# First group of a hybrid decoder step, layer 0: the norm factor moves from the input to the evictions, and its statistic behind the first unit of products

## The chip, the core and the metric

The kernel runs on one core of one Trainium2 chip. The metric is the device time of one execution in microseconds; the median of three runs before the change is 2014.07 us (2012.44 to 2017.64).

## The reference, cut to what matters

The reference makes one inference step of a two-layer decoder for 1024 prompt tokens and 64 sample tokens. Layer 0, the one that is changed, is

```python
proj = rms_norm(x, norm_g) @ w_in            # x * rsqrt(mean(x*x) + EPS) * g
u, gb, gc, q_mem, z = split(proj)
conv = sum(conv_w[j] * full[:, j:j+t] for j in range(3))   # full: history, then gc * u
q = rms_norm(q_mem, mem_q_g)                 # per head
out = concat(gb * conv, mem_attend(q, k, v)) * silu(z)
y = x + out @ w_out
```

The keys and values of the memory, for both layers, come from `rms_norm(mem, norm_g) @ w_kv`. Layer 1 (latent attention) has the same shape of input projection and is not changed.

## The kernel before, in words

**Products.** All large products are made in three passes: `split` (L183, L179) cuts each operand into a high half on ScalarE and a low half on VectorE (or POOL), and `mm3` (L188 to L191) adds high by high, high by low and low by high in PSUM. Data lie with features on the partitions and tokens in the free dimension. Group A has 320 tokens (256 of the prompt and the 64 samples), group B the other 768 in two chunks of 384. A unit is 128 output features: eight steps of the contraction in `fm`, three products each, so 24 products per chunk. A PSUM tile for it comes from a ring of three (`mmt`).

**Weights.** `Stream` loads the weights of a unit on SP's queue, splits them, and keeps two units in both forms; `get(i)` splits unit i + 1 and issues the load of i + 2. The first unit comes in four pieces (L297). For the memory weights (`mem_kv`, 8 units of 2048 columns over two layers) `M_ENG` names the engine of the low half unit by unit: `"vvgv"` gives units 2 and 6 to POOL, the others to VectorE.

**Group A, layer 0** (`group_a`). Four DMAs load `x`. `norm_T` squares the eight blocks on ScalarE (L250, L258), adds them on VectorE (L259), then `norm_T2` takes the statistic: `stat_r` sums over partitions on TensorE (L214), scales on VectorE (L220), and finds the inverse root by an integer guess and three Newton steps of tiny instructions (`rsqrt_`, L202 to L206). `bcast_tok` puts the factor on a diagonal (L233) and multiplies it with ones on TensorE (L234), so that PSUM holds the factor of each token on all partitions. Each block is then scaled (`xnxa`, L272) and split into `xH` and `xL` (L183, L179). Only then can `in0` make its first product.

`in0` runs over 40 units: conv blocks 0 to 3 of four units each (`u`, gc, z, gb), then four memory heads of two units each (`mem_part`: query and gate), then conv blocks 4 to 7, with the attention of the samples over their memory beside them. In a conv block, `u` is copied out of PSUM on ScalarE (L654), gc is multiplied with it (L659), three multiply-adds make the convolution `cv`, z is turned into its gate by `silu2` (tanh on ScalarE, L608, and one instruction on VectorE, L609), `cv` is multiplied by it (L678), and gb by that (L682). In layer 1 the same helpers already work with a factor `rb` that is multiplied in at the eviction: L605 in `silu2`, L452 for the query's sum of squares, and `split_g` (L239, L240) makes the halves of the input with the gain but without the factor.

**Order.** Two streams of work are written by generators, and `interleave` merges them by the costs that they yield: on the left `mem_kv`, group B, prompt attention and the end; on the right group A, then the samples' attention. A right cost is multiplied by 0.8 in the first part (`RAT`), by 0.6 from the memory heads of group A on. So at the start `mem_kv` (5.2 for its first unit, then 2.6 per half unit) is merged with group A: the squares yield 0.48 each, the statistic `NY` = 7.0, the broadcast 3.0, the eight scaled blocks 0.64 each, and a unit 3.2. Group B's squares, statistic and scaled blocks come after `mem_kv`, beside group A's memory heads. The merged order sets priorities; a planner then puts the instructions on each engine's queue, where they run in order.

Of the kernel before, what the change touches and what calls it, by code (L numbers as in the profile page):

```python
# [5 lines left out]
F = mybir.dt.float32  # L6
# [5 lines left out]
AF = mybir.ActivationFunctionType  # L12
ALU = mybir.AluOpType
# [3 lines left out]
D = 1024  # L17
# [7 lines left out]
EPS = 1e-6  # L25
# [23 lines left out]
KL = list(range(6, 12)) + list(range(6))  # L49
NATB = 4  # L50
RECB = 2
M_ENG = ("vvgv", "a")
A_ENG = ("v", "a")
SCL = "vaaaaaaa"
PSP = "ggg"
# [2 lines left out]
NY = 7.0  # L58
# [27 lines left out]
VG0, VG1, VGM, VGQL, VGQ, VGK, VMQ, VCW = 0, 8, 16, 32, 35, 36, 37, 39  # L86
# [6 lines left out]
def build(nc, tc, I, O):  # L93
# [94 lines left out]
    def mm3(out, wh, wl, xh, xl, first, last):  # L188
        T.matmul(out, wh, xh, start=first, stop=False)  # L189
        T.matmul(out, wh, xl, start=False, stop=False)  # L190
        T.matmul(out, wl, xh, start=False, stop=last)  # L191

    cnt = [0]
    sm = {}
# [43 lines left out]
    def split_g(h, l, x, c):  # L238
        A.activation(h, x, AF.Copy, scale=vcol(c))  # L239
        V.scalar_tensor_tensor(out=l, in0=x, scalar=vcol(c), in1=h.bitcast(F), op0=ALU.mult, op1=ALU.subtract)  # L240
# [87 lines left out]
    def fm(ps, n, w, nk, xH, xL, c0):  # L328

        wh, wl = w  # L330
        for k in range(nk):
            mm3(ps[:, 0:n], wh[:, k * 128:(k + 1) * 128], wl[:, k * 128:(k + 1) * 128], xH[:, k, c0:c0 + n], xL[:, k, c0:c0 + n], k == 0, k == nk - 1)


    def mem_kv(side=None):
# [90 lines left out]
    def mem_part(l, g, pp, ws, qi, xH, xL, ydst, done, pq, rb=None, fill=None):  # L426
# [9 lines left out]
        def qpart(h, d):  # L436

            assert sm["kv"] >= l
            kr = pp.tile([128, 512], F, name="mraw", tag="mraw", bufs=1)
            S.dma_start(out=kr[:, 0:256], in_=d_kT[l][:, h, :])  # L440
            S.dma_start(out=kr[:, 256:512].rearrange("p (k d) -> p k d", k=2), in_=d_v[l][:, :, h * 128:(h + 1) * 128])
            qH = pp.tile([128, g.np], R, name="mqH", tag="mqH", bufs=2 if g.sample else 1)
            qL = pp.tile([128, g.np], R, name="mqL", tag="mqL", bufs=2 if g.sample else 1)
            sqt = pp.tile([128, g.T], F, name="msq", tag="msq", bufs=1)
            w = ws.get(qi + 2 * h)
            for c0, n in g.chunks:
                ps = mmt()
                fm(ps, n, w, 8, xH, xL, c0)
                yield 0.01 * n
                A.activation(sqt[:, c0:c0 + n], ps[:, 0:n], AF.Square)  # L450
                if l:
                    V.scalar_tensor_tensor(out=sqt[:, c0:c0 + n], in0=acc1[g][:, c0:c0 + n], scalar=EPS * 128 / D, in1=sqt[:, c0:c0 + n], op0=ALU.mult, op1=ALU.add)  # L452
                m = max(0, min(n, g.np - c0))
                split(qH[:, c0:c0 + m], qL[:, c0:c0 + m], ps[:, 0:m], "a", "v")
                if m < n:
                    A.activation(QZ[:, :, 40 * h:40 * h + 8], ps[:, m:n].rearrange("p (b t) -> p b t", t=8), AF.Copy, scale=vcol(VMQ + l))
                    for gg in range(2):
                        o = SQ[:, gg, :].rearrange("p (b h t) -> p b h t", h=4, t=8)[:, :, h, :]
                        V.tensor_copy(o, sqt[:, g.np + 32 * gg:g.np + 32 * gg + 32].rearrange("p (b t) -> p b t", t=8))
            w = ws.get(qi + 2 * h + 1)  # L460
            kH = pp.tile([128, 512], R, name="mkH", tag="mkH", bufs=2)
            kL = pp.tile([128, 512], R, name="mkL", tag="mkL", bufs=2)
            split(kH, kL, kr, "a", MKE)
            y = yd[h] = ydst(h)
            for j, (c0, n) in enumerate(g.chunks):
                ps = mmt()
                fm(ps, n, w, 8, xH, xL, c0)
                if j == 0:
                    st = pst("x", "mst")
                    for i in range(nt):  # L470
                        T.matmul(st[:, 2 * i:2 * i + 2], sqt[:, i * 128:(i + 1) * 128], ones[:, 0:2], start=True, stop=True)
                yield 0.01 * n
                silu2(pp, y[:, c0:c0 + n], ps, n, rb[:, c0:c0 + n] if l else None)
                if j == 0:
                    v = pp.tile([128, nt], F, name="mv_", tag="mv_")
                    rs = pp.tile([128, nt], F, name="mrs", tag="mrs", bufs=2)
                    V.tensor_scalar(out=v, in0=st[:, 0:2 * nt].rearrange("p (i two) -> p i two", two=2)[:, :, 0], scalar1=1.0 / 128, scalar2=EPS * EPS if l else EPS, op0=ALU.mult, op1=ALU.add)
                    rsqrt_(pp, rs, v, [128, nt])
                    V.tensor_scalar(out=rs, in0=rs, scalar1=MSC, scalar2=None, op0=ALU.mult)
            d.update(h=h, kH=kH, kL=kL, qH=qH, qL=qL, rs=rs)  # L480
# [57 lines left out]
    def samples(l, g, pp, nb):  # L538
# [14 lines left out]
        for gg in range(2):  # L553
# [1 line left out]
            T.matmul(st[:, 0:2], SQ[:, gg, :], ones[:, 0:2], start=True, stop=True)  # L555
            v = pp.tile([128, 1], F, name="smv", tag="smv")
            r = pp.tile([128, 1], F, name="smr", tag="smr")
            V.tensor_scalar(out=v, in0=st[:, 0:1], scalar1=1.0 / 128, scalar2=EPS * EPS if l else EPS, op0=ALU.mult, op1=ALU.add)
            rsqrt_(pp, r, v, [128, 1])
            V.tensor_scalar(out=r, in0=r, scalar1=MSC, scalar2=None, op0=ALU.mult)  # L560
            load(8 * gg + 3)
# [63 lines left out]
    kpesT = pc.tile([NS, NS], F, name="kpesT")  # L625


    def in0(g, xH, xL, ytile, done, pq, last=None):
        P = Pools(g.side)
        pw = P.new("p1w" + str(g.p0))  # L630
        order = [u + 8 * (u > 15) for u in range(4 * HB)] + list(range(16, 24)) + list(range(4 * HB + 8, 40))
# [12 lines left out]
        def conv(cb, u0, pp):  # L644
            vb = pp.tile([128, 2 + g.np + (80 if g.sample else 0)], F, name="vb", tag="vb", bufs=2)
            u = pp.tile([128, T_], F, name="u", tag="u", bufs=1)
            cv = pp.tile([128, T_], F, name="cv", tag="cv", bufs=1)
            G.tensor_copy(vb[:, 0:2], hist[:, cb, :])
            if g.sample:
                vs = vb[:, 2 + g.np:].rearrange("p (b w) -> p b w", w=10)  # L650
                G.tensor_copy(vs[:, :, 0:2], stc[:, cb])
            for c0, n, ps in prod(u0):
                yield 0.01 * n
                A.activation(u[:, c0:c0 + n], ps[:, 0:n], AF.Copy)  # L654
            for c0, n, ps in prod(u0 + 1):
                yield 0.01 * n
                m = max(0, min(n, g.np - c0))
                if m:
                    V.tensor_tensor(out=vb[:, 2 + c0:2 + c0 + m], in0=ps[:, 0:m], in1=u[:, c0:c0 + m], op=ALU.mult)  # L659
                if m < n:  # L660
                    V.tensor_tensor(out=vs[:, :, 2:10], in0=ps[:, m:n].rearrange("p (b t) -> p b t", t=8), in1=u[:, c0 + m:c0 + n].rearrange("p (b t) -> p b t", t=8), op=ALU.mult)
            parts = [(cv[:, 0:g.np], [vb[:, j:j + g.np] for j in range(3)])]
            if g.sample:
                parts.append((cv[:, g.np:].rearrange("p (b t) -> p b t", t=8), [vs[:, :, j:j + 8] for j in range(3)]))
                G.tensor_copy(newc[:, cb, 2:18].rearrange("p (b w) -> p b w", w=2), vs[:, :, 8:10])
                G.tensor_copy(hist[:, cb, :], vb[:, g.np:g.np + 2])
            else:
                G.tensor_copy(newc[:, cb, 0:2], vb[:, g.np:g.np + 2])
            for o, vv in parts:
                cw = [vcol(VCW + 3 * cb + j) for j in range(3)]  # L670
                V.tensor_scalar(out=o, in0=vv[0], scalar1=cw[0], scalar2=None, op0=ALU.mult)
                V.scalar_tensor_tensor(out=o, in0=vv[1], scalar=cw[1], in1=o, op0=ALU.mult, op1=ALU.add)
                V.scalar_tensor_tensor(out=o, in0=vv[2], scalar=cw[2], in1=o, op0=ALU.mult, op1=ALU.add)
            s2 = pp.tile([128, T_], F, name="s2", tag="u", bufs=1)
            for c0, n, ps in prod(u0 + 2):
                yield 0.01 * n
                silu2(pp, s2[:, c0:c0 + n], ps, n)
            V.scalar_tensor_tensor(out=cv, in0=s2, scalar=0.5, in1=cv, op0=ALU.mult, op1=ALU.mult)  # L678
            y = ytile(cb)
            for c0, n, ps in prod(u0 + 3):  # L680
                yield 0.01 * n
                V.tensor_tensor(out=y[:, c0:c0 + n], in0=cv[:, c0:c0 + n], in1=ps[:, 0:n], op=ALU.mult)  # L682
            done(cb, y)
# [7 lines left out]
            yield "S"  # L691
        pm = P.new("p1m" + str(g.p0))
        nxt = conv(half, 8 + 4 * half, pp) if g.sample else None
        yield from mem_part(0, g, pm, ws, 4 * half, xH, xL, lambda h: ytile(8 + h), lambda h, y: done(8 + h, y), pq, None, nxt)
        P.close(1)
        if g.sample:
            pms = P.new("psm0")
# [949 lines left out]
    def group_a(g, xin):  # L1647
# [9 lines left out]
        x = pt.tile([128, 8, g.T], F, name="x")  # L1657
        for k in range(0, 8, 2):
            S.dma_start(out=x[:, k:k + 2, :], in_=xin[:, k:k + 2, :])
        yield from norm_T(pt, x, VG0, g.tiles, g.T, xH, xL, "xa")  # L1660
        L.close(1)
        py = L.new("pya")
        yraw = [py.tile([128, g.T], F, name=f"yr{b}") for b in range(12)]
        pq = L.new("pqa")
        yield from in0(g, xH, xL, lambda b: yraw[b], lambda b, y: None, pq)
        L.close(1)
        xH, xL = halves()

# [283 lines left out]
```

## Time and profile before

| | |
|---|---|
| median of three runs | 2014.07 us (2012.44 to 2017.64) |
| the profiled execution | 2021.16 us |
| its span, first to last instruction | 2019.4 us |
| mean granted TensorE clock | 0.980 |
| TensorE busy | 1918.3 us, 12508 products |
| VectorE / ScalarE / POOL busy | 983.4 / 744.7 / 474.6 us |

The rows below come from this one execution. Times are microseconds from the start of the span unless marked ns. PE is TensorE, PEld its weight loads, DVE VectorE, ACT ScalarE, POOL GpSimd, SP the queue that issues DMAs. A busy share is read by stage, since different stages have different limits; idle time of an engine matters where the end of the work hangs on it. PEclk 1.00 is 2.4 GHz and 0.50 is 1.2 GHz.

### The profile page before, as it was taken

The page shows a single profiled execution, that of the slowest core. Times are in us where ns is not written, and L with a number is a line of the kernel's source. Part 1 is how long each engine was busy: PE and PEld are TensorE (multiplying, and loading weights), DVE is VectorE, ACT ScalarE, POOL GpSimd, SP SyncE. Part 2 cuts the span into 40 slices and gives each one's busy share as a digit, 9 for nine tenths or more (in the row PEclk, how much of TensorE's full clock was granted, in tenths as well). Part 3 has the DMA queues.
Part 4 walks back from the last instruction along what each step waited for, and adds up shares of the span by engine and source line. Part 5 has one row for each costly group of instructions (what it writes and reads, how often), then busy time and mean ns, then how long its engine had stood idle before and what let it go on. Part 6 is the DMA issues. An engine that isn't in the chain of part 4 may idle for free. (4 is left out here: it accounts for less than half of the span.)

```text
span 2019.4 us, 35704 instructions
## 1 busy us (share of the span) xinstructions
PE 1918.3 (95%) x12508; PEld 1653.9 (82%) x12508; DVE 983.4 (49%) x2673; ACT 744.7 (37%) x1499; POOL 474.6 (24%) x493
## 2 busy tenths in 40 slices
PE   6998999999999999999999999999998899998999
PEld 5997998999997877777787766777787787787999
DVE  7659535456544434434322543444446656656300
ACT  6445223334311233323222422333333666666300
POOL 1200000000000233323433324333332443432120
PEclk8999999999999999999999989999999999999999
DMA  5563535433544688678997879877852211213532
GB/s 202 193 207 124 165 131 194 145 117 114 181 160 140 194 266 270 221 249 281 321 314 260 292 235 301 255 240 231 284 156 67 84 58 56 67 40 129 183 95 72
DMA packets 192884, 368.28 MB, mean 182 GB/s; under 512 B 27809, under 2 KB 135585, under 8 KB 191426
## 3 DMA queue, kind: packets, MB, share of 16 engines
q1 hardware_dynamic: 172178, 298.75, 45.5%
q0 software_dynamic: 20528, 67.26, 10.3%
q8 instruction: 99, 1.62, 0.3%
q14 instruction: 79, 0.65, 0.1%
HBM read 331.22 MB, written 34.70 MB: 181 GB/s over the span
## 5 line engine op out<-in xcount | busy, mean ns | idle before, releaser
L1078 POOL DMA_INDIRECT nat<-nat,IX x256 | 270.6, 1057 | 517.9 <-PE pv L1163 451.6
L189 PE MATMUL mm<-xH,whi 128*128 128x384 f32 (+1 forms) x1112 | 369.1, 332 | 6.5 <-ACT whi L183 6.5
L191 PE MATMUL mm<-xH,wli 128*128 128x384 f32 (+1 forms) x1112 | 364.0, 328 | 1.8 <-DVE wli L179 1.8
L190 PE MATMUL mm<-xL,whi 128*128 128x384 f32 (+1 forms) x1112 | 364.0, 327 | 0.0
L189 PEld LDWEIGHTS mm<-xH,whi 128*128 128x128 f32 x1112 | 211.6, 190 | 22.5 <-issue 10.0
L183 ACT ACTIVATE whi<-wri 128x1024 fp32r<-128x1024 f32 (+1 forms) x130 | 126.4, 979 | 278.2 <-PE mm L190 228.4
L190 PEld LDWEIGHTS mm<-xL,whi 128*128 128x128 f32 x1112 | 211.4, 190 | 3.0 <-issue 2.8
L191 PEld LDWEIGHTS mm<-xH,wli 128*128 128x128 f32 x1112 | 211.1, 190 | 3.3 <-DVE wli L179 2.6
L179 DVE TENSOR_TENSOR wli<-wri,whi 128x1024 fp32r<-128x1024 f32 (+1 forms) x130 | 147.0, 1136 | 123.9 <-ACT whi L183 122.6
L1163 PE MATMUL pv<-nat,PT 128*64 128x256 f32 x1024 | 141.0, 397 | 16.6 <-ACT PT L1143 13.8
L1092 PE MATMUL sAB<-rec,qar 128*64 128x256 f32 x1024 | 150.4, 389 | 1.9 <-DVE mx L1107 1.6
L1163 PEld LDWEIGHTS pv<-nat,PT 128*64 128x64 f32 x1024 | 76.6, 140 | 60.6 <-ACT PT L1143 21.3
L1092 PEld LDWEIGHTS sAB<-rec,qar 128*64 128x64 f32 x1024 | 79.4, 138 | 45.5 <-issue 12.8
L1107 DVE CUSTOM_DVE_ANT_1 ss<-sAB,rec,mx 128x256 f32<-128x256 f32 x120 | 57.9, 483 | 113.3 <-PE sAB L1097 68.8
L189 PE MATMUL mm<-nH,whi 128*128 128x384 f32 x304 | 104.8, 345 | 1.1 <-ACT mP L497 1.0
L190 PE MATMUL mm<-nL,whi 128*128 128x384 f32 x304 | 102.7, 338 | 0.1
L191 PE MATMUL mm<-nH,wli 128*128 128x384 f32 x304 | 102.2, 336 | 0.0
L189 PE MATMUL mm<-yHo,who 128*128 128x384 f32 (+1 forms) x288 | 96.9, 337 | 1.3 <-ACT yHo L183 1.3
L191 PE MATMUL mm<-yHo,wlo 128*128 128x384 f32 (+1 forms) x288 | 94.2, 327 | 0.0
L190 PE MATMUL mm<-yLo,who 128*128 128x384 f32 (+1 forms) x288 | 93.9, 326 | 0.0
L183 ACT ACTIVATE who<-wro 128x768 fp32r<-128x768 f32 (+3 forms) x44 | 38.1, 873 | 146.7 <-PE mm L190 115.5
L1434 ACT ACTIVATE ass<-ass,anb,arq 128x128 f32<-128x128 f32 (+3 forms) x64 | 55.4, 866 | 63.6 <-DVE anb L1432 63.6
(588 smaller groups left out, 4196.3 us busy)
## 6 DMA issues: line engine op xcount, KB each, us to landing
rec<-rec SPq DMA_DIRECT2D x512, 192.0 KB
wri<-wi SPq DMA_DIRECT2D x114, 512.0 KB
wro<-wo SPq DMA_DIRECT2D x29, 384.0 KB
smkv<-ckm SPq DMA_DIRECT2D x16, 512.0 KB
smkv<-cvm SPq DMA_DIRECT2D x16, 512.0 KB
wrm<-memw SPq DMA_DIRECT2D x7, 1024.0 KB
wro<-wo SPq DMA_DIRECT2D x7, 768.0 KB
yld<-d_ys SPq DMA_DIRECT2D x8, 544.0 KB
```

Source lines behind the costliest of these rows:

```text
L179: eng.tensor_tensor(out=out, in0=a, in1=h.bitcast(F), op=ALU.subtract)
L183: A.activation(h, src, AF.Copy)
L189: T.matmul(out, wh, xh, start=first, stop=False)
L190: T.matmul(out, wh, xl, start=False, stop=False)
L191: T.matmul(out, wl, xh, start=False, stop=last)
L1078: G.indirect_dma_start(out=t[:, j % 2, :], out_offset=None, in_=I["nat"], in_offset=bass.IndirectOffsetOnAxis(ap=IX[:, q:q + 1], axis=0), ...
L1092: T.matmul(s[x][64 * ab:64 * ab + 64, 0:256], QA[:, cb, b, :], part(t, cb * 128 + ab * 64)[:, 4 * x:4 * x + 4, :], start=(cb == 0), stop=F ...
L1107: V.tensor_tensor_reduce(out=ss[:, 256 * x:256 * x + 256].rearrange("p (g k) -> p g k", g=4), in0=s[x][:, 0:256].rearrange("p (g k) -> p g ...
L1163: T.matmul(d["v"][64 * ab:64 * ab + 64, 0:256], PT[:, j, ab, :], n[j][:, ab * 256:ab * 256 + 256], start=(i == 0 and j == 0), stop=(i == C ...
L1434: A.activation(ss[:, 0:kv], ss[:, 0:kv], AF.Exp, bias=nb, scale=d["rq"][:, i:i + 1], accum_out=ls)
```

## The change

Group A's input in layer 0 is split with the gain alone, without the norm factor, as soon as it has landed; its squares are taken beside that into `acc1[g]`. The factor's statistic and broadcast become a function `scales`, which `in0` calls in its first conv block after the products of the first unit; `tc.issue_after` puts its TensorE instructions behind the last of these products (`sm["fm"]`) on the queue. It writes the factor `rb` and its square `rb2` to SBUF on ScalarE. The factor is multiplied in where the products leave PSUM: `u` takes the square (on VectorE, in place of the copy on ScalarE), which serves u and gc both; z is multiplied in `silu2`, `cv` once more by `rb` for gb. The memory heads take the paths that layer 1 has. The costs yielded are 0.96 for each of the eight blocks and `NY` after the statistic. The low halves of memory units 2 and 6 go from POOL to VectorE. Group B is unchanged.

```diff
-M_ENG = ("vvgv", "a")
+M_ENG = ("vvvv", "a")
...
-        T.matmul(out, wl, xh, start=False, stop=last)
+        return T.matmul(out, wl, xh, start=False, stop=last)
...
-            mm3(ps[:, 0:n], wh[...], wl[...], xH[:, k, c0:c0 + n], xL[:, k, c0:c0 + n], k == 0, k == nk - 1)
+            m = mm3(ps[:, 0:n], wh[...], wl[...], xH[:, k, c0:c0 + n], xL[:, k, c0:c0 + n], k == 0, k == nk - 1)
+        sm["fm"] = m.ins
...
@@ mem_part and samples: the paths of layer 1 @@
-                if l:
+                if rb is not None:
                     V.scalar_tensor_tensor(out=sqt[:, c0:c0 + n], in0=acc1[g][:, c0:c0 + n], scalar=EPS * 128 / D, in1=sqt[:, c0:c0 + n], op0=ALU.mult, op1=ALU.add)
-                silu2(pp, y[:, c0:c0 + n], ps, n, rb[:, c0:c0 + n] if l else None)
+                silu2(pp, y[:, c0:c0 + n], ps, n, None if rb is None else rb[:, c0:c0 + n])
...
@@ in0, conv @@
-                A.activation(u[:, c0:c0 + n], ps[:, 0:n], AF.Copy)
+                if rb is None:
+                    A.activation(u[:, c0:c0 + n], ps[:, 0:n], AF.Copy)
+                else:
+                    if cb == 0:
+                        with tc.issue_after(sm["fm"]):
+                            scales()
+                        yield NY
+                    V.tensor_tensor(out=u[:, c0:c0 + n], in0=ps[:, 0:n], in1=rb2[:, c0:c0 + n], op=ALU.mult)
...
-                silu2(pp, s2[:, c0:c0 + n], ps, n)
+                silu2(pp, s2[:, c0:c0 + n], ps, n, None if rb is None else rb[:, c0:c0 + n])
             V.scalar_tensor_tensor(out=cv, in0=s2, scalar=0.5, in1=cv, op0=ALU.mult, op1=ALU.mult)
+            if rb is not None:
+                V.tensor_tensor(out=cv, in0=cv, in1=rb, op=ALU.mult)
...
@@ group_a @@
-        yield from norm_T(pt, x, VG0, g.tiles, g.T, xH, xL, "xa")
+        rb, rb2 = [px.tile([128, g.T], F, name=n) for n in ("rb0", "rbq")]
+        acc = acc1[g]
+        for k in range(8):
+            split_g(xH[:, k, :], xL[:, k, :], x[:, k, :], VG0 + k)
+            if k == 0:
+                A.activation(acc, x[:, 0, :], AF.Square)
+            else:
+                sq = pt.tile([128, g.T], F, name="sqxa", tag="sq", bufs=2)
+                A.activation(sq, x[:, k, :], AF.Square)
+                V.tensor_tensor(out=acc, in0=acc, in1=sq, op=ALU.add)
+            yield 0.003 * g.T
+
+        def scales():
+            r = stat_r(px, [acc], g.tiles, D, "xa")[1]
+            for c0, n, ps in bcast_tok(px, r, g.tiles, g.T, "xa"):
+                A.activation(rb[:, c0:c0 + n], ps[:, 0:n], AF.Copy)
+                A.activation(rb2[:, c0:c0 + n], ps[:, 0:n], AF.Square)
```

## Rows read from the trace of the kernel before

**Rows 1.** The page, part 1: busy time, share of the span and instructions of TensorE (PE), of its weight loads (PEld) and of VectorE (DVE).

```profile
PE 1918.3 (95%) x12508; PEld 1653.9 (82%) x12508; DVE 983.4 (49%) x2673; ACT 744.7 (37%) x1499; POOL 474.6 (24%) x493
```

**Rows 2.** Busy time of each engine by stage, in stretches of 50 us: length, busy us and instructions of PE, PEld, DVE, ACT, POOL, then the granted TensorE clock, the DMA share and GB/s.

```profile
0.00:50.00 50.00, 31.86 (x179) 29.69 (x180) 37.58 (x98) 30.10 (x75) 9.60 (x16) 0.83 0.57 201
50.00:100.00 50.00, 50.00 (x380) 49.84 (x380) 32.29 (x69) 24.44 (x44) 10.19 (x10) 1.00 0.57 195
100.00:150.00 50.00, 47.18 (x329) 46.49 (x329) 29.60 (x67) 21.68 (x32) 4.15 (x8) 0.97 0.62 211
150.00:200.00 50.00, 40.42 (x262) 38.27 (x261) 45.99 (x135) 28.12 (x56) 1.33 (x6) 0.92 0.38 116
```

**Rows 3.** The same view, cut at the waits of the first 50 us.

```profile
16.00:26.00 10.00, 8.01 (x51) 7.64 (x51) 8.94 (x19) 9.15 (x29) 3.07 (x5) 0.83 0.94 333
26.00:36.18 10.18, 2.35 (x12) 1.87 (x12) 7.67 (x18) 3.48 (x10) 4.41 (x2) 0.63 0.33 125
36.18:42.20 6.02, 6.02 (x26) 6.02 (x27) 6.02 (x15) 4.75 (x10) 0.00 (x0) 0.50 0.00 0
```

**Rows 4.** Who waited for whom, TensorE only, 26 to 50 us: engine and line, the releaser, us in total, times, longest.

```profile
PE bcxa L234 <- DVE dgxa L233: 5.9, 1, 5.9
PE mm L189 <- ACT whi L183: 1.9, 1, 1.9
PE mm L189 <- ACT u L654: 0.5, 1, 0.5
PE mm L191 <- DVE wli L179: 0.5, 1, 0.5
```

**Rows 5.** The timeline of 25 to 36.5 us, all engines: start, us, engine and line, what is written and read, and in brackets the idle time before and its releaser.

```profile
25.76 0.78 PE L214 MATMUL statxa<-ones,sqaxa 128*128 128x2 f32 x6 [0.53 <-DVE sqaxa L259]
25.76 4.65 POOL L179 TENSOR_TENSOR wlm<-wrm,whm 128x1024 fp32r<-128x1024 f32 x2 [4.72 <-ACT whm L183]
...
26.83 1.31 DVE L202 TENSOR_SCALAR strxa<-stvxa 128x3 int32<-128x3 int32 x1
...
28.17 2.25 DVE L204 TENSOR_TENSOR rsq<-strxa 128x3 f32<-128x3 f32 x1
30.43 0.33 SPq L297 DMA_DIRECT2D wrm<-memw  x1
30.46 0.16 DVE L205 SCALAR_TENSOR_TENSOR rsq<-rsq,stvxa 128x3 f32<-128x3 f32 x1
...
34.31 1.01 DVE L272 SCALAR_TENSOR_TENSOR xnxa<-x,vec,bcxa 128x320 f32<-128x320 f32 x2 [0.80 <-PE bcxa L234]
...
36.18 0.64 PE L189 MATMUL mm<-xH,whi 128*128 128x320 f32 x1 [1.91 <-ACT whi L183]
```

**Rows 6.** Prices: single lines of the views of one tile or one source line, each with minimum, median and maximum in ns, the first and last start in us, and the shapes.

```profile
L272 DVE SCALAR_TENSOR_TENSOR xnxa<-x,vec,bcxa x8: 539/540/548, 34.3 to 41.7; 128x320 f32<-128x320 f32 x8
...
L179 DVE TENSOR_TENSOR xL<-xnxa,xH x8: 481/484/486, 36.4 to 45.2; 128x320 fp32r<-128x320 f32 x8
...
L240 DVE SCALAR_TENSOR_TENSOR xL<-xr,vec,xH x8: 544/546/552, 336.0 to 393.4; 128x320 fp32r<-128x320 f32 x8
...
L605 DVE TENSOR_TENSOR ym<-mm,rb x12: 483/554/558, 463.5 to 1414.5; 128x384 f32<-128x384 f32 x8, 128x320 f32<-128x320 f32 x4
L844 ACT ACTIVATE rb<-bcn x3: 383/439/597, 430.9 to 1192.4; 128x320 f32<-128x320 f32 x1, 128x512 f32<-128x512 f32 x1, 128x256 f32<-128x256 f32 x1
...
L452 DVE SCALAR_TENSOR_TENSOR msq<-acc,msq x12: 483/552/558, 456.9 to 1398.4; 128x384 f32<-128x384 f32 x8, 128x320 f32<-128x320 f32 x4
...
L678 DVE SCALAR_TENSOR_TENSOR cv<-s,cv x16: 484/718/958, 61.4 to 917.2; 128x320 f32<-128x320 f32 x8, 128x768 f32<-128x768 f32 x8
...
L654 ACT ACTIVATE u<-mm x12: 415/419/492, 47.1 to 295.7; 128x320 f32<-128x320 f32 x8, 128x384 f32<-128x384 f32 x4
```

**Rows 7.** The timeline of 76 to 100 us, first VectorE, then POOL.

```profile
79.78 1.22 DVE L179 TENSOR_TENSOR wli<-wri,whi 128x1024 fp32r<-128x1024 f32 x1
...
84.94 2.53 DVE L179 TENSOR_TENSOR wli<-wri,whi 128x1024 fp32r<-128x1024 f32 x1 [3.62 <-ACT whi L183]
...
81.62 4.77 POOL L179 TENSOR_TENSOR wlm<-wrm,whm 128x1024 fp32r<-128x1024 f32 x2 [0.45 <-ACT whm L183]
```

**Rows 8.** Groups of VectorE's instructions from 16 to 26 us: line, what is written and read, count, busy us, mean ns.

```profile
L240 DVE SCALAR_TENSOR_TENSOR memL<-memx,vec,memH 128x256 fp32r<-128x256 f32 x6 | 2.9, 482 | 0.0
```

**Rows 9.** Who waited for whom, TensorE only, 16 to 26 us.

```profile
PE mm L189 <- ACT whm L183: 1.4, 1, 1.4
PE mm L190 <- DVE wlm L179: 1.0, 1, 1.0
PE statxa L214 <- DVE sqaxa L259: 0.5, 1, 0.5
```

**Rows 10.** Groups of VectorE's instructions from 126 to 205 us.

```profile
L272 DVE SCALAR_TENSOR_TENSOR xnxb<-x,vec,bcxb 128x512 f32<-128x512 f32 (+1 forms) x16 | 9.5, 607 | 0.0
L179 DVE TENSOR_TENSOR xL<-xnxb,xH 128x768 fp32r<-128x768 f32 x8 | 7.6, 952 | 0.1
```

**Rows 11.** Who waited for whom, TensorE only, 120 to 200 us.

```profile
PE mtr L512 <- DVE mP L500: 4.6, 2, 3.1
PE my L189 <- ACT mPTH L183: 1.9, 2, 1.2
...
PE sst L555 <- DVE mPTL L179: 1.5, 1, 1.5
```

More of the change, by code (lines that the diff above doesn't have):

```diff
@@ L331, in fm @@
         for k in range(nk):
-            mm3(ps[:, 0:n], wh[:, k * 128:(k + 1) * 128], wl[:, k * 128:(k + 1) * 128], xH[:, k, c0:c0 + n], xL[:, k, c0:c0 + n], k == 0, k == nk - 1)
+            m = mm3(ps[:, 0:n], wh[:, k * 128:(k + 1) * 128], wl[:, k * 128:(k + 1) * 128], xH[:, k, c0:c0 + n], xL[:, k, c0:c0 + n], k == 0, k == nk - 1)
+        sm["fm"] = m.ins
     def mem_kv(side=None):
@@ L476, in qpart @@
                     rs = pp.tile([128, nt], F, name="mrs", tag="mrs", bufs=2)
-                    V.tensor_scalar(out=v, in0=st[:, 0:2 * nt].rearrange("p (i two) -> p i two", two=2)[:, :, 0], scalar1=1.0 / 128, scalar2=EPS * EPS if l else EPS, op0=ALU.mult, op1=ALU.add)
+                    V.tensor_scalar(out=v, in0=st[:, 0:2 * nt].rearrange("p (i two) -> p i two", two=2)[:, :, 0], scalar1=1.0 / 128, scalar2=EPS if rb is None else EPS * EPS, op0=ALU.mult, op1=ALU.add)
                     rsqrt_(pp, rs, v, [128, nt])
@@ L557, in samples @@
             r = pp.tile([128, 1], F, name="smr", tag="smr")
-            V.tensor_scalar(out=v, in0=st[:, 0:1], scalar1=1.0 / 128, scalar2=EPS * EPS if l else EPS, op0=ALU.mult, op1=ALU.add)
+            V.tensor_scalar(out=v, in0=st[:, 0:1], scalar1=1.0 / 128, scalar2=EPS * EPS, op0=ALU.mult, op1=ALU.add)
             rsqrt_(pp, r, v, [128, 1])
@@ L625, in build, with in0 @@
     kpesT = pc.tile([NS, NS], F, name="kpesT")
-    def in0(g, xH, xL, ytile, done, pq, last=None):
+    def in0(g, xH, xL, ytile, done, pq, last=None, rb=None, rb2=None, scales=None):
         P = Pools(g.side)
@@ L693, in in0 @@
         nxt = conv(half, 8 + 4 * half, pp) if g.sample else None
-        yield from mem_part(0, g, pm, ws, 4 * half, xH, xL, lambda h: ytile(8 + h), lambda h, y: done(8 + h, y), pq, None, nxt)
+        yield from mem_part(0, g, pm, ws, 4 * half, xH, xL, lambda h: ytile(8 + h), lambda h, y: done(8 + h, y), pq, rb, nxt)
         P.close(1)
@@ L1664, in group_a @@
         pq = L.new("pqa")
-        yield from in0(g, xH, xL, lambda b: yraw[b], lambda b, y: None, pq)
+        yield from in0(g, xH, xL, lambda b: yraw[b], lambda b, y: None, pq, None, rb, rb2, scales)
         L.close(1)
```

## The prediction

> **What bounds the kernel now.** First the page's totals [rows 1]: TensorE is busy 95% of the span, VectorE 49%. So time goes where TensorE idles or runs at half clock, and the table of stages says where that is early on [rows 2]: in the first 50 us TensorE has 31.9 busy us at a granted clock of 0.83, in 50 to 100 it has no gap, and in 150 to 200 it has 40.4 with VectorE at 46.0 of 50. The first stretch and the one from 150 on are those that this change can move; 50 to 150 is nearly full.
>
> A finer cut of the first stretch [rows 3]: from 26 to 36.18 us TensorE is busy 2.35 of 10.18 us, 7.83 idle, and the next 6.02 us run at clock 0.50, that is at 1.2 GHz, the lower level. The list of waits gives the owner [rows 4]: 5.9 us for the diagonal tile `dgxa` (L233), 1.9 for the first weight half (L183), 0.5 each for an eviction and a low half. In the timeline [rows 5] this is one chain: statistic products of group A at 25.76, the inverse root on VectorE (L202 at 26.83, L204 to L206 after it), the diagonal and the broadcast, the first scaled blocks `xnxa` at 34.31, their high halves on ScalarE, and the first product of group A at 36.18. Nothing else was ready, since memory unit 2, whose low half POOL makes from 25.76 to 30.41, stands behind that first product on TensorE's queue.
>
> Two steps of the chain are stretched: L202 takes 1.31 us and the first L204 2.25 us, where the later steps take 0.16. They end at 28.14 and 30.42, and POOL's two low halves fill 25.76 to 30.41.
>
> **What the change does, part by part.**
>
> *Removed at the head.* The 8 `xnxa` (0.540) and 8 `xL` (0.484) on VectorE [rows 6], 8.2 us; ScalarE's 8 `xH` stay as scaled copies. Above all the chain of rows 5 no longer stands before the first product.
>
> *Added at the head.* 8 low halves of the other form, multiply and subtract in one; layer 1 has that very form at 320 columns: 0.546 [rows 6], 4.4 us, now needed before the first product and beside the 7 additions of squares. The low half of memory unit 2 comes to VectorE: 2 x 1.22 = 2.4 (the price of the same piece on VectorE, [rows 7]), in place of 2 x 2.33 on POOL.
>
> *When can TensorE go on?* VectorE is busy 8.94 us between 16 and 26 [rows 3]. Six `memL` of the second memory layer lie in there (6 x 0.482 = 2.9, [rows 8]) and can wait. Needed by then: 8.94 - 2.9 + 4.4 + 1.22 (half of unit 2's low part) = 11.7, and 1.06 us in which it waited for products: 16 + 12.7 = 28.7. I take 28.7 as the time at which products flow, instead of 36.18: 7.5 earlier. But the 2.35 busy us that lay in the gap (statistic and broadcast) are still to be done: **5.1 us** gained. Ends: 2.5, if VectorE keeps the order of before and the `memL` stay ahead, and 7.8, if group A's first unit fills the whole gap.
>
> *The clock.* 6.02 us at half rate cost 3.0. Between 16 and 26, with waits of 1.4, 1.0 and 0.5 us on TensorE [rows 9], the granted clock was 0.83 [rows 3], so short idling still brings it down for a while. I take half: **1.5**, ends 0 and 3.0. The Trainium skill ("TensorE: Matmul & The Clock Gate", section "Part 1: The HAM clock gate (the "warmup" mystery)") speaks against that half: the throttled rate is the default and only activity lifts it, so by it a remaining gap leaves the clock down, and the sum below would be 5.1; the row at 0.50 behind the gap agrees with it, the row at 0.83 shows both levels within ten us.
>
> *Small waits* behind the first product (0.5 and 0.5, [rows 4]): half of them, **0.5**; ends 0 and 1.0.
>
> *The chain in its new place.* It stands behind unit 0's 24 products, and its end holds unit 0's eviction, and with it one of three PSUM tiles, on which unit 1 waits. Length: from the statistic's end, 25.76 + 0.78, to 34.31 it is 7.8 [rows 5]; less what the two stretched steps have over 0.16 (1.15 + 2.09), 4.5; plus two ScalarE evictions at 0.439 [rows 6], 5.4 us. Cover: the 48 products of memory unit 2 or 3. From 50 to 100 us TensorE makes 380 products in 50 us without a gap [rows 2], 0.13 each, so 48 are 6.3 us, about the chain's length. I take **0**; if the cover is gone it is 5.4. Queued behind the wait on VectorE: the eviction of `u` and what follows; SP's weight loads wait for the splits, which do not wait for the chain. SP loses a wait: its load of memory unit 4 was released at 30.43 by POOL's end [rows 5], and will now follow VectorE.
>
> *Evictions.* Eight `u` go from ScalarE (0.419) to VectorE with the squared factor: 0.483, the price of L605, which reads PSUM and a factor alike (the least of its group, the 320-column form, here and below; [rows 6]). Each of 8 conv blocks gains a multiply in the gate (0.483) and one of `cv` by the factor (0.484, the price of L678); each of 4 memory heads gains a gate multiply and a sum of squares with the scaled statistic (0.485, L452). VectorE gains 8 x 1.45 + 4 x 0.97 = 15.5 us over some 270. In 50 to 100 it is busy 32.3 of 50 [rows 2]; if all four blocks that stand before the heads and unit 6's low half fell there, that would be 32.3 + 5.8 + 2.4 = 40.5: hidden, price 0. Bounds: 0, and the whole of what falls where VectorE is full.
>
> *That place* is 126 to 205 us: group B's norm runs there (16 `xnxb`, 8 `xL`, 17.1 us of VectorE, [rows 10]) beside the four heads of group A, and TensorE waits 4.6 us for `mP`, 1.9 for `mPTH`, 1.5 for `mPTL` and more [rows 11]. Four heads (3.9) and two conv blocks (2.9) add 6.8 there at most. VectorE has 4.0 us free in 150 to 200. And the order shifts: the planner's costs of group A's head fall from 7 x 0.48 + 7 + 3 + 8 x 0.64 = 18.5 to 8 x 0.96 + 7 = 14.7, times 0.8 it is 3.0 earlier than the left stream, 1.2 units. So one head more is over before group B's scaling begins, and conv units take its place. I take **-0.5**; ends -6.8 and +2.
>
> *Unit 6's low half* (second use of POOL): POOL's 4.77 us from 81.62 made one `wli` take 2.53 instead of 1.22 [rows 7]. VectorE gains 2.44 and loses 1.3 of blocking, while TensorE has no gap: 0.
>
> *POOL* has nothing queued behind the two removed pieces that a product waits for: 0. DMAs are unchanged in number and size; they start earlier.
>
> **Sum.** 5.1 + 1.5 + 0.5 - 0.5 = 6.6 us. The profiled execution took 2021.16 (span 2019.4 and 1.8 around it), so 2014.6 for one like it; it lies 7.1 above the median of the runs, 2014.07, which gives **2007.5**. A measurement of this kernel can tell about 0.3%, 6 us, from no change.
>
> **Rivals.**
>
> *The clock stays down and part of the gap remains.* Products resume near 30, not 28.7, as VectorE works off splits in the old order, and run at 1.2 GHz again. For it: VectorE is at 8.9 of 10 us before the gap [rows 3]. Gain 5.1 - 1.3 + 0.5 - 0.5 = 3.8, some 2010. Chance 0.2, within 0.3%.
>
> *The wait is only moved.* Unit 0 waits for its weights, the chain comes behind it, unit 1 finds no PSUM tile, and TensorE waits for the eviction of `u` where it waited for `dgxa`. For it: three tiles, of which the memory units take two at a time. Against: the shortened chain is about as long as a memory unit. Price 5.4 of the 6.6: about 2013. Chance 0.2, also if the change does not do what it says, the queue placing unit 0 behind memory unit 2 so that the statistic comes later than before.
>
> *Slower: VectorE is the bound in group B's norm.* At 126 to 205 us the 6.8 us land in front of `mP` and `mPTL` and, since one engine takes its work in order, all come out as waits of TensorE, with half-rate stretches after them (clock 0.92 in 150 to 200, [rows 2]) for another 3. With a head that gives 3 it is 2014 + 6.8 + 3 - 3, about 2021. It decides once VectorE's free 4.0 us are used up and the shift by 1.2 units brings no relief. Against: the head that moves out takes some 4 us with it. Chance 0.1.
>
> **Numbers.** The forecast's case, with its own range 2001 (idle 7.8, clock 3.0, waits 1.0, and 1 from the shift, 12.8 in all) to 2008, has 0.5. The two cases within 0.3% have 0.4 together, the slower one 0.1. So faster by over 0.3%: 0.5, within: 0.4, slower: 0.1. The range of 2001 to 2018 takes in the best head and a good part of the slow case; 8 in 10 should lie in it. The whole order of instructions is planned anew from the changed costs, which may move later waits by a few us either way; that is in the range too.
>
> **What would show it.** Right: no wait for `dgxa` above 1 us, products of memory unit 2 before 30 us, the granted clock in 30 to 50 above 0.8, TensorE's busy time in the first 50 us near 38, the eviction of `u` at L654's place on VectorE with no product waiting for it. The steps L202 and L204 at 0.16. In 150 to 200, TensorE at 40 or more. Wrong: a new wait of 3 us or more for `u` or for `xL` in the first 50 us; TensorE below 39 in group B's norm with VectorE at 48 or more; or a head that is 6 us shorter and a later stage that gives it back, seen as the same group of products starting as late as before.

## The result, and the profile after

The changed kernel takes **2039.67 us** (median of 6 runs, 2036.17 to 2049.29) against 2015.86 for the kernel before on the same chip: ratio **1.0131**, 95% interval 1.0096 to 1.0166. It is slower by some 26 us (the ratio; 23.8 between the medians) where 6.6 us of gain were forecast. Its profiled execution took 2047.6 us (span 2045.8), 26.4 more than that of before. The page's totals:

```profile
PE 1924.7 (94%) x12508; PEld 1653.1 (81%) x12508; DVE 992.7 (49%) x2701; ACT 742.5 (36%) x1493; POOL 456.7 (22%) x489
```

The count of products is unchanged, VectorE has 28 instructions and 9.3 busy us more, ScalarE and POOL have less. No other engine became the bound of the whole: VectorE stays at 49% of the span. Of the 26.4 us, 20.0 are idle time of TensorE (2045.8 - 1924.7 against 2019.4 - 1918.3), the rest is longer busy time for the same products. In what follows, "lost" is TensorE's idle time in a stretch plus (1 - granted clock) times its busy time; the clock has two digits, which alone makes a lost time uncertain by about a quarter of a us per 50 us. The traces come from several chips. Four of the experiments below keep the order of before up to 200 us; their traces lose 23.1 to 23.4 us in the first 50 us, where that of before loses 23.6, and 16.8 to 19.1 in 100 to 200, where it loses 17.0. Stages as in [rows 2], of the changed kernel:

```profile
0.00:50.00 50.00, 32.62 (x199) 31.17 (x200) 38.88 (x111) 33.06 (x78) 6.83 (x18) 0.90 0.67 236
50.00:100.00 50.00, 50.00 (x379) 49.79 (x379) 31.59 (x63) 22.20 (x39) 2.10 (x6) 1.00 0.51 170
100.00:150.00 50.00, 47.85 (x335) 47.30 (x334) 33.02 (x82) 22.44 (x34) 2.92 (x6) 0.97 0.61 213
150.00:200.00 50.00, 41.22 (x267) 39.51 (x267) 44.27 (x127) 24.66 (x47) 1.75 (x6) 0.93 0.37 117
200.00:250.00 50.00, 46.21 (x279) 45.60 (x278) 28.77 (x62) 14.60 (x19) 2.41 (x9) 0.93 0.48 154
```

The first stage lost 17.4 idle + 3.3 slow = 20.6 us, before 18.1 + 5.4 = 23.6 [rows 2]: a gain of 3.0, not 7. Up to 200 us the changed kernel is ahead by 4.7 us of lost time. Then it gives it back: the stage from 200 had 50.00 of 50 busy before. The head in detail, first by stretches as in [rows 3], then the waits of 0 to 60 us in the form of [rows 4]:

```profile
16.00:26.00 10.00, 0.97 (x9) 0.77 (x7) 9.35 (x19) 9.04 (x22) 2.99 (x4) 0.81 0.99 353
26.00:32.00 6.00, 4.16 (x15) 3.96 (x16) 6.00 (x13) 6.00 (x17) 0.00 (x0) 0.50 0.20 63
...
32.00:50.00 18.00, 18.00 (x138) 17.77 (x137) 15.07 (x61) 6.81 (x16) 1.82 (x4) 0.99 0.51 185
```

```profile
PE mm L189 <- ACT whi L183: 10.9, 1, 10.9
PE mm L189 <- ACT whm L183: 6.4, 2, 6.1
```

The wait for `dgxa` (5.9) is gone, as forecast. But from 16 to 26 us, where TensorE was busy 8.01 us [rows 3], it is now busy 0.97: one wait of 10.9 us, for the first weights of group A. The timeline (columns as in [rows 5]) says why:

```profile
25.82 0.46 ACT L1678 ACTIVATE sqxa<-x 128x320 f32<-128x320 f32 x1
26.43 1.05 ACT L183 ACTIVATE whm<-wrm 128x1024 fp32r<-128x1024 f32 x1
27.38 1.32 ACT L183 ACTIVATE whi<-wri 128x256 fp32r<-128x256 f32 x4
27.84 0.63 PE L189 MATMUL mm<-xH,whi 128*128 128x320 f32 x1 [10.86 <-ACT whi L183]
...
33.60 0.71 PE L214 MATMUL statxa<-ones,acc 128*128 128x2 f32 x6
34.24 0.39 PE L189 MATMUL mm<-whm,memH 128*128 128x256 f32 x1
34.88 0.15 DVE L202 TENSOR_SCALAR strxa<-stvxa 128x3 int32<-128x3 int32 x1
35.07 0.16 DVE L204 TENSOR_TENSOR rsq<-strxa 128x3 f32<-128x3 f32 x1
...
40.23 0.49 DVE L662 TENSOR_TENSOR u<-mm,rbq 128x320 f32<-128x320 f32 x1 [1.28 <-ACT rbq L1687]
```

TensorE's queue is now: memory unit 0, group A's unit 0, the statistic, memory unit 1. Before, both memory units (96 products in 95 rows) stood ahead of group A. Memory unit 1's products ran from 16 us on before [rows 3]; now unit 0 stands in front of them and waits for its weights, whose high half is split at 27.38. ScalarE makes that half, and it has no gap from 22.21 us on: group A's high halves `xH` and squares (the last square at 25.82) and memory weights (26.43) stand ahead of it. The chain behind unit 0 runs from 33.60 to 40.23 with TensorE busy 18.00 of 18.00 us beside it.

The rest of the loss lies far behind the edit. Stretches 500 to 550 and 600 to 700 us, first of the kernel before, then of the changed one:

```profile
500.00:550.00 50.00, 48.98 (x318) 48.52 (x317) 25.90 (x54) 16.96 (x30) 1.18 (x5) 1.00 0.54 177
600.00:700.00 100.00, 99.29 (x574) 81.12 (x573) 47.77 (x106) 19.64 (x29) 14.25 (x13) 1.00 0.50 158
```

```profile
500.00:550.00 50.00, 44.24 (x273) 43.33 (x272) 21.20 (x48) 14.58 (x26) 0.71 (x3) 0.93 0.47 158
600.00:700.00 100.00, 96.13 (x516) 79.61 (x516) 43.45 (x95) 17.15 (x26) 11.29 (x13) 0.95 0.40 133
```

Lost time: 1.0 and 0.7 us before, 8.9 and 8.7 after. These two holes are 15.9 us of the 26.4 between the two traces; the other stretches of 100 us differ by 6.2 at most, some one way and some the other. Not one instruction there was edited; in 440 to 560 us this is group A's layer 1, in 600 to 700 its samples and what follows. The longest TensorE waits of the changed kernel in 440 to 560 us, then in 600 to 700:

```profile
PE mtr L513 <- DVE mP L501: 4.0, 1, 4.0
PE my L189 <- ACT mPTH L183: 3.5, 4, 1.0
```

```profile
PE mm L962 <- DMA swk<-wuk: 2.0, 1, 2.0
PE smo L587 <- ACT whi L183: 0.9, 1, 0.9
PE mm L1031 <- ACT qnT L1015: 0.7, 1, 0.7
```

Before, the longest was 1.0 us in the first stretch, and in the second a single wait of 0.7 for the same load of weights, `swk`. What did change there is the order in which the two streams are merged.

### The profile page after: what moved, and what is told of

The parts are those of the page before. It is cut to its first block, busy times and chain, and to the rows that moved or that the text cites. A ratio compares the mean times of both kernels' runs of the same rounds, so it can differ in the third digit from the quotient of the medians.

```text
span 2045.8 us, 35725 instructions
## 1 busy us (share of the span) xinstructions
PE 1924.7 (94%) x12508; PEld 1653.1 (81%) x12508; DVE 992.7 (49%) x2701; ACT 742.5 (36%) x1493; POOL 456.7 (22%) x489
## 5 line engine op out<-in xcount | busy, mean ns | idle before, releaser
L1088 POOL DMA_INDIRECT nat<-nat,IX x256 | 265.6, 1038 | 537.1 <-PE pv L1173 459.4
L189 PEld LDWEIGHTS mm<-xH,whi 128*128 128x128 f32 x1112 | 213.6, 192 | 29.5 <-ACT whi L183 14.9
L1173 PE MATMUL pv<-nat,PT 128*64 128x256 f32 x1024 | 143.1, 405 | 15.1 <-ACT PT L1153 14.9
```

What stands on the lines that cost most here:

```text
L1088: G.indirect_dma_start(out=t[:, j % 2, :], out_offset=None, in_=I["nat"], in_offset=bass.IndirectOffsetOnAxis(ap=IX[:, q:q + 1], axis=0), ...
L1173: T.matmul(d["v"][64 * ab:64 * ab + 64, 0:256], PT[:, j, ab, :], n[j][:, ab * 256:ab * 256 + 256], start=(i == 0 and j == 0), stop=(i == C ...
```

## The experiments

Three groups, each on one chip with its own 19 to 22 runs of the kernel before (median 2011.47, 1996.36 and 2011.78 us), so ratios are compared, and 1% is 20 us. The question of the first group: does the loss come from the merged order, from the places of the new tiles, or from the new work itself?

**Costs only.** The kernel before, with the yield of group A's statistic lowered by what the change takes off that step's sum (18.5 to 14.7; 3.8 x 0.8 = 3.04 cost units on the scale on which the two streams are compared). No instruction is added or removed.

```diff
-        yield NY
+        yield NY - (3.8 if tag == "xa" else 0.0)
```

> The kernel before, with the cost yielded after group A's statistic lowered by 3.8 (7.0 to 3.2), so that the right stream runs as far ahead of the left as in the changed kernel; no instruction is added or taken away. Theory M (the new merge of the two streams loses the time later on): slower than before by 15 to 30 us, some 2030 to 2045. Theory V (the added work of VectorE at the evictions loses it): within 6 us of before. Theory S (the SBUF that the factor's two tiles take in group A's pool loses it): within 6 us of before.

Measured 2034.19 us, ratio 1.0105 (1.0068 to 1.0141): about +21 us with the kernel's work untouched. Its waits in 440 to 560 us have the same wait of 4.0 us, and its stages the same holes:

```profile
PE mtr L512 <- DVE mP L500: 4.0, 1, 4.0
```

```profile
500.00:550.00 50.00, 44.24 (x276) 43.49 (x276) 21.43 (x43) 13.90 (x22) 1.18 (x5) 0.97 0.49 165
600.00:700.00 100.00, 96.22 (x523) 77.54 (x522) 43.88 (x92) 16.68 (x24) 11.76 (x13) 0.95 0.43 137
```

**Tiles' places.** The changed kernel with the factor tiles, and the diagonal, as slices of the idle `olT`, so that group A's pools are as before.

```diff
-        rb, rb2 = [px.tile([128, g.T], F, name=n) for n in ("rb0", "rbq")]
+        fl = olT.rearrange("p a b t -> p (a b t)")
+        rb, rb2 = fl[:, 0:g.T], fl[:, g.T:2 * g.T]
...
```

> The changed kernel, with the factor, its square and the diagonal kept in a tile that lies idle until the samples' attention (olT), so that group A's pool is as large as before (but for a few bytes). Theory S: the loss goes, some 2005 to 2012. Theories M and V: as the changed kernel, some 2035 to 2045.

Measured 1.0124 (1.0073 to 1.0174): nothing comes back. The theory of the places falls.

**Places and order back.** The same, and the step's old sum of cost behind `scales()`.

```diff
-                        yield NY
+                        yield NY + 3.8
```

> The same with 3.8 added to the cost yielded behind the statistic, so that every unit from the second on is merged with the left stream where it was before the change. Theory M: the loss goes and the gain of the head stays, some 2005 to 2012. Theory V: as the changed kernel, 2030 to 2045. Theory S: as the run with the SBUF as before, 2005 to 2012.

Measured 0.9989 (0.9966 to 1.0012): the whole loss is gone, with all of the change's arithmetic in place. But the gain of the head does not show either: unit 0 still stands ahead of memory unit 1, TensorE waits 11.3 us for `whi`, and the first 50 us lose 23.0 us (its stages 0 to 50 and 150 to 200):

```profile
0.00:50.00 50.00, 31.39 (x201) 29.67 (x202) 39.09 (x111) 32.90 (x78) 5.51 (x14) 0.86 0.68 239
150.00:200.00 50.00, 39.64 (x253) 37.42 (x252) 46.89 (x135) 27.15 (x55) 0.64 (x3) 0.91 0.39 116
```

**Low halves only.** The kernel before with `M_ENG = ("vvvv", "a")`.

> The kernel before, with only the low halves of memory units 2 and 6 moved to VectorE. All three theories: within 6 us of before; by the prediction's prices the head gains up to 3 us, since the two stretched steps of the inverse root go back to 0.16 us, some 2011 to 2015.

Measured 0.9993 (0.9971 to 1.0015): worth nothing that can be told, though its first 50 us lose 20.5, as little as the changed kernel's.

The second group asked **where** the order costs, by shifting it by the same 3.04 cost units in one stretch only, in the kernel before. A yield of -5.07 (x 0.6) behind the layer 0 memory heads begins the shift at about 205 us; +5.07 there ends the one of the costs-only kernel; -4.05 (x 0.75, the rate of that part) behind `yield "B"` begins it with group A's layer 1.

```diff
             yield from nxt
+            yield -5.07
```

> The kernel before with the merge shifted by 5.07 cost units (3.8 without the stretch's scale) only from group A's layer 0 memory heads on (about 205 us); no instruction added or removed. Theory late: the loss of the cost-only run (+21 us) comes from what lies behind 205 us, the layer 1 memory heads without cover among it (wait on mP 4.0): 2027 to 2036. Rival early: the loss comes from group B's norm and first matrix beside it, 35 to 205 us: 2008 to 2015.

Measured 1.0131 (1.0095 to 1.0167): the loss is there, a little above the upper end of what was expected (on the 2011.47 us of the first group 1.0131 is 2037.8).

```diff
+        yield NY - (3.8 if tag == "xa" else 0.0)
...
             next(sg)
+            yield 5.07
```

> The cost-only run with the 5.07 cost units given back at group A's layer 0 memory heads, so that the merge is shifted in 35 to 205 us alone. Theory late: 2010 to 2016. Rival early: 2027 to 2036.

Measured 0.9989 (0.9975 to 1.0002): the shift beside group B's norm, 35 to 205 us, costs nothing.

```diff
         yield "B"
+        yield -4.05
```

> The kernel before with the merge shifted by about the same amount only from group A's layer 1 on (behind the point where it meets group B at the layer's end, about 440 us). If the loss lies in the layer 1 memory heads and what follows: 2025 to 2036, with the wait of 4.0 on mP in 440 to 560 us. If it needs the shift in layer 0's scan and second half too: 2009 to 2020, and then that wait is short.

Measured 1.0140 (1.0108 to 1.0171), with the same 4.0 us for `mP`. So all of the order's cost lies behind some 440 us. In the same group ran the kernel in which the head should work as forecast:

**Unit 0 behind both memory units.** The changed kernel with tiles in `olT`, the step's old cost (7.0 + 3.8 = 10.8) yielded ahead of unit 0 and none behind the statistic.

```diff
+        yield 10.8
...
         yield from in0(...)
...
-                        yield NY
+                        yield 0.0
```

> The changed kernel with the factor tiles in idle memory of group A, the step's old total of cost, and 10.8 cost units yielded ahead of the unit 0 products, so that both memory units of products (95) stand on TensorE's queue ahead of group A's first product, as before the change. Theory place: the idle 10.9 us at the head is there only because unit 0 stands ahead of memory unit 1; here 16 to 26 us is filled again, TensorE's lost time by 100 us is 15 to 18 (before 23.6, the changed kernel 20.6), and the whole is 2003 to 2008, 4 to 8 us under the run with unit 0 ahead. Rival, the first matrix's weights or PSUM end the wait anyway: lost time by 100 us 20 or more and the whole 2010 to 2014.

Measured 1990.61 us, ratio **0.9974** (0.9960 to 0.9988), about 5 us faster than the kernel before on its chip, and the lowest ratio of the study. Its first 50 us, with TensorE's waits from 16 to 50 us:

```profile
0.00:50.00 50.00, 37.69 (x245) 36.24 (x246) 42.55 (x121) 36.30 (x83) 4.93 (x17) 0.93 0.77 269
```

```profile
PE mm L189 <- ACT kscr L390: 3.8, 1, 3.8
PE mm L190 <- DVE wlm L179: 1.1, 1, 1.1
```

Lost 12.3 + 2.6 = 14.9 us, 8.6 less than before; the wait for `whi` is gone. What is late next is ScalarE again: a memory product waits 3.8 us until the squares of the keys (L390) have been taken out of PSUM, which ScalarE does behind group A's `xH` and squares. Part of the gain seems not to last: in 100 to 200 us, beside group B's norm, this version loses 20.9 us, against 17.0 before and 19.1 at most in the four traces with its order.

```profile
100.00:150.00 50.00, 46.51 (x311) 45.45 (x309) 33.07 (x81) 23.99 (x38) 2.70 (x5) 0.93 0.62 211
150.00:200.00 50.00, 39.81 (x245) 37.98 (x246) 46.00 (x133) 24.58 (x46) 0.96 (x5) 0.90 0.37 114
```

Whether the new work at the evictions or the order there takes it was not separated.

The third group cut once more, and applied the finding to the change itself.

**The change, late order back.** The changed kernel as it is, with 5.07 yielded behind the layer 0 heads.

> The changed kernel as it is, with 5.07 cost units yielded behind group A's layer 0 memory heads, so that only the order from about 205 us on is that of before; tile places, head order and early order stay changed. Theory late (all of the loss lies in the order behind 205 us, and the rest of the change is worth about nothing as long as unit 0 stands ahead of the second memory unit): 0.997 to 1.003 of the kernel before. Rival, the tiles' places or the early order cost as well: 1.006 or more.

Measured 1.0005 (0.9987 to 1.0023): one yield that emits no instruction takes the 1.3% away.

**Unit 0 behind half a unit.** 7.3 ahead of unit 0 and 3.5 behind the statistic.

> As the run with unit 0 behind the memory products, but with 7.3 cost units ahead of the unit 0 products, so that they are merged into the second memory unit's products behind its first 14. TensorE has work from 16 us on as there: lost time by 100 us 14 to 18, the whole 0.996 to 0.999 of before. If the place of the statistic among the products matters (it stands one unit's products later or earlier), up to 0.003 apart from the other run.

Measured 0.9980 (0.9962 to 0.9998). The time is as expected, the head is not: lost 20.3 us, since unit 0's first product stands behind 24 products of memory unit 1 (the expectation said 14) and still waits for its weights:

```profile
PE mm L189 <- ACT whi L183: 6.0, 1, 6.0
```

So the two versions with a later unit 0 can't be told apart by time, though their heads differ by 5 us. Nor can either be told from the run with places and order back, whose head loses 23.0 us: 0.9989 (0.9966 to 1.0012) overlaps both. What unit 0's place is worth at the end is not shown to better than that.

**Shift in the layer 1 heads only**, and **behind them only**: -4.05 behind `yield "B"` and +4.05 behind `in1_mem`; or -4.05 behind `in1_mem` alone.

```diff
         yield from in1_mem(g, ws, pp, xH, xL, pq, rb)
         N.close(1)
+        if g.sample:
+            yield 4.05      # or -4.05, without the one at "B"
```

> The kernel before with the merge shifted by 4.05 cost units from group A's layer 1 on, as in the run that cost 1.4%, but given back right behind the layer 1 memory heads (about 440 to 560 us shifted). Theory, every stage pays for its own order: the wait of 4.0 on mP with the half clock behind it stays, 5 to 10 us lost in 500 to 550, the whole 1.002 to 1.006 of before. Rival, the heads are the cause of all that follows (a delay there is carried on): 1.010 or more.

Measured 1.0059 (1.0034 to 1.0084). Its two stretches:

```profile
500.00:550.00 50.00, 44.23 (x273) 43.49 (x272) 19.90 (x43) 13.03 (x22) 0.71 (x3) 0.97 0.49 158
600.00:700.00 100.00, 99.15 (x584) 82.57 (x573) 49.49 (x109) 20.06 (x31) 14.25 (x13) 1.00 0.49 160
```

> The same shift, begun only behind group A's layer 1 memory heads (about 560 us on). Theory, every stage pays for its own order: 500 to 550 as before (1 us idle), the idle time and half clock of 600 to 700 and what follows stay: 1.006 to 1.011 of before. Rival, the heads are the cause of all: 0.998 to 1.003.

Measured 1.0083 (1.0054 to 1.0113). Its two stretches:

```profile
500.00:550.00 50.00, 48.98 (x319) 48.43 (x319) 25.77 (x53) 18.37 (x32) 1.18 (x5) 1.00 0.54 174
600.00:700.00 100.00, 96.23 (x523) 76.85 (x521) 43.40 (x92) 16.66 (x24) 12.04 (x13) 0.95 0.43 139
```

Each shift makes the hole of its own stretch and leaves the other's as before, and 0.59% + 0.83% = 1.42% agrees with the 1.40% of both. In these two runs every stage pays for its own order; no delay is carried on.

**How one hole comes about.** Product by product, the last head of group A's layer 1, TensorE then VectorE. The heads-only kernel:

```profile
516.53 0.28 PE L191 MATMUL msc<-mkH,mqL 128*128 128x256 f32 x1
520.77 0.63 PE L512 MATMUL mtr<-ident,mP 128*128 128x128 f32 x4 [3.96 <-DVE mP L500]
```

```profile
516.85 0.69 DVE L493 TENSOR_REDUCE mmx<-msc 128x2 f32<-128x512 f32 x1 [0.15 <-PE msc L191]
517.46 1.22 DVE L179 TENSOR_TENSOR wli<-wri,whi 128x1024 fp32r<-128x1024 f32 x1
518.59 0.15 DVE L494 SCALAR_TENSOR_TENSOR mnb<-mmx,mrs 128x2 f32<-128x2 f32 x1
520.07 0.17 DVE L498 RECIPROCAL mls<-mls 128x2 f32<-128x2 f32 x1 [1.33 <-ACT mP L497]
520.27 0.61 DVE L500 TENSOR_SCALAR mP<-mP,mls 128x256 f32<-128x256 f32 x2
```

And the kernel before:

```profile
513.85 0.28 PE L191 MATMUL msc<-mkH,mqL 128*128 128x256 f32 x1
513.97 0.34 PE L189 MATMUL mm<-xH,whi 128*128 128x384 f32 x1
...
516.99 0.34 PE L191 MATMUL mm<-xH,wli 128*128 128x384 f32 x1
517.17 0.63 PE L512 MATMUL mtr<-ident,mP 128*128 128x128 f32 x4
```

```profile
514.27 0.68 DVE L493 TENSOR_REDUCE mmx<-msc 128x2 f32<-128x512 f32 x1
514.98 0.16 DVE L494 SCALAR_TENSOR_TENSOR mnb<-mmx,mrs 128x2 f32<-128x2 f32 x1
```

Scores, their softmax on VectorE and ScalarE, and the transposes of `mP` are a chain of about 3 us. In the kernel before, products of group B and of the head before stand between scores and transposes on TensorE's queue, so it has no gap. In the shifted order nothing stands there, and on VectorE a low half of weights (1.22 us) has slipped between the maximum and the next step. TensorE waits 3.96 us and then runs at 1.2 GHz for some us: the granted clock is 0.50 in 523 to 524 us and 1.00 again from 525.4 on, which makes the 0.97 of the whole stretch.

```profile
523.00:524.00 1.00, 1.00 (x6) 1.00 (x5) 0.00 (x0) 0.00 (x0) 0.00 (x0) 0.50 0.02 8
```

## Why the prediction was wrong

**The step that failed** is the last sentence of "Numbers": that the newly planned order "may move later waits by a few us either way". The shift itself had been worked out rightly (18.5 to 14.7, times 0.8, 3.0 cost units), but its effect was followed only as far as group B's norm, and there it was counted as a relief, inside a term that took off 0.5 us; what lies behind had no term in the sum. In fact the 3.04 cost units stay in the merge, since nothing in `interleave` takes a shift out again, and by themselves cost about 21 us (1.0105, costs only), three times the forecast gain. They cost nothing that shows up to 205 us (0.9989) and everything behind: 0.59% in the layer 1 heads, 0.83% behind them. Taken out behind 205 us alone, they take the loss with them (1.0005). Of some 12 us that the heads take, the stages 450 to 550 show 7.9 as lost time (5.8 + 1.3 against 1.0 in the second, 2.5 against 0.7 idle in the first). Which stages take the rest stays open, and so does why the load `swk` and the two shorter waits come late at 600 to 700. The range, too, ended at 2018, below the price of the prediction's own slower rival (about 2021). Only this one size and direction of shift was run: that another shift would cost as much, or that one would gain, is not shown.

**"When can TensorE go on?"** is a second step that failed in the run: idle time in the first 50 us fell by 0.8 us (18.1 to 17.4) where 5.1 and 0.5 were forecast. It gave 28.7 us, and products flow again at 27.84, but that agreement is partly luck. The 28.7 was added up from VectorE's work alone, and the wait that ended last was for ScalarE, whose queue the sum left out. The sum also took for granted that memory unit 1 still fills 16 to 26 us. That is the first half of the second rival (unit 0 waits for its weights): the wait moved, from 5.9 for `dgxa` and 1.9 for `whi` to 10.9 for `whi`. Its second half, a missing PSUM tile, did not come. The signs named for being wrong were a wait for `u` or `xL`, and the wait came at a tile they did not name. With unit 0 behind both memory units the forecast of the head holds in size: TensorE busy 37.69 us in the first 50 ("near 38"), the granted clock 0.93, 8.6 us less lost against 7.1 forecast for the three terms. The whole of that version is 5 us (2 to 8) faster.

**The clock.** The half-rate stretch that stood behind the gap [rows 3] did not go away, it moved to 26 to 32 us (0.50), behind the new gap, with 4.16 busy us in it where 6.02 were; from 32 us on it is 0.99. In the first stage the clock term is 5.4 to 3.3, 2.1 us against 1.5. That a gap leaves the lower rate behind it is what the Trainium skill says ("TensorE: Matmul & The Clock Gate", section "Part 1: The HAM clock gate (the "warmup" mystery)": the throttled rate is the default, activity lifts it); the row of 26 to 32 us agrees with it.

**Right in size:** the chain in its new place at 0 (from the statistic's end at 34.31 to 40.23, 5.9 us against 5.4, TensorE full beside it); the steps L202 and L204 at 0.15 and 0.16 once POOL is idle beside them (1.31 and 2.25 before, [rows 5]; 0.17 and 0.16 in the run that moves the low halves alone); the low halves of units 2 and 6 together at nothing that can be told (0.9993, 0.9971 to 1.0015). The evictions near 0: with all of them in place and the order of before, the ratio is 0.9989 (0.9966 to 1.0012).

**The slower rival** had the right sign for the wrong reason. VectorE did not become the bound in 126 to 205 us: TensorE has 41.22 busy us in 150 to 200 ("40 or more") and VectorE 44.27, less than the 45.99 of before. With the order of before and all evictions in place VectorE is at 46.89 and TensorE at 39.64 there, and the whole still is 0.9989. The prediction named a sign that is near to what came, "a later stage that gives it back", but gave that no price, and here the head was only 3.0 us shorter and the later stages lost far more.

## What to carry to other kernels

Where a cost model or a list of yields sets the order of two merged streams, an edit that changes a cost moves every later meeting of the two: price the shift by itself, by running the old kernel with the new costs alone, and give the step its old sum of cost before judging what the edit is worth. When a step is moved on a queue, write down the queue before and after and ask for each instruction that now stands further ahead when its own operands come; here the ready work was put behind work that was not. For the step that will make the waiting engine go on, add up the work of every engine that feeds it, here ScalarE too. A gap that closes in its stage is not yet as much at the end: here 8.6 us at the head stood beside 5 (2 to 8) of the whole.

## What the runs showed of the hardware

An added or altered yield, which emits no instruction, moved the time by 1.0 to 1.4% in three kernels, and by 0.6 and 0.8% in the two that shift one stretch. In the two stretches shown, the price is idle time of TensorE (3.8 to 5.8 us) and, behind it, time at the lower clock (1.3 to 4.8 us more, idle and lower clock counted as above). Two steps of 128x3 on VectorE took 1.31 and 2.25 us beside POOL's low halves, and 0.17 and 0.16 us with these low halves moved away and nothing else changed.
